# A two-layer decoder trunk on one core: the first norm's row sums by matmul, sixteen hand-over transfers split seven to nine, and the query projection with both activation parts in one 512-column matmul

## The chip, the cores and the metric

The kernel runs on one core of a Trainium2 chip. The metric is device time in microseconds of one execution. Engines are named as in the profile: PE is the matmul engine (PEld its weight loads), DVE the vector engine, ACT the scalar engine, POOL is GpSimd, SP the engine that only issues transfers (POOL and ACT issue some too). A row "L316" points at line 316 of the kernel before.

## The reference, cut to what matters

One sequence of 256 tokens, width 2048, fp32, passes two layers:

```python
for l in range(DEPTH):                    # DEPTH = 2
    h = rms_norm(x, mix_norm[l])
    if l % 2 == 0:
        h = mixer_ab(h, ...)              # gated spatial mixing, and a gated linear recurrence (HGRN2)
    else:
        h = mixer_c(h, ...)               # attention with forget gates, 16 heads
    x = x + h
    h = rms_norm(x, ffn_norm[l])
    x = x + conv_ffn(h, ...)              # up-projection, width-3 causal convolution, SiLU gate, down-projection

def rms_norm(x, gain):
    y = x * lax.rsqrt(jnp.mean(x * x, axis=-1, keepdims=True) + RMS_EPS)
    return y * gain
```

In `mixer_ab` one input projection of the normed x yields six parts u, v, q, f, i, g of 1024 columns each. In the recurrence, each of 8 heads of 128 has queries q, keys from f, values from i; its scores are formed per chunk with a running decay. The division by the root mean square is a factor per token, so the kernel applies it after the projections (except in q, whose scale goes out in the later head norm together with a factor on the outputs).

## The kernel before, in words

**Layout and number format.** x is kept feature-major: 16 tiles `xT[k]` of 128 features x 256 tokens. Every projection is computed to nearly fp32 accuracy from two reduced-precision parts: an operand w is split into `wh` (rounded to the matmul format, by ACT) and `wl = w - wh` (by DVE), and an activation tile `a` of 512 columns holds its high part in columns 0 to 255 and its low part in 256 to 511 (`split`). A product is the sum of three matmuls: high x high, low weight x high activation, high weight x low activation. Weights stream from memory in pieces of 128x1024, 512 KB each, issued on SP and split as they land (`weights`, `halves`, lines 185 and 186); three to five buffers let this run ahead of PE.

**Two kinds of projection.** `project_four` (lines 360 to 362), `project_tok` and `project_first` (lines 260 and 236) keep tokens as rows: the activation is the loaded weight of PE, and 512 columns of the weight matrix stream by. `project` (line 316) keeps features as rows: 128 columns of the weight matrix are loaded, and 256 token columns stream by. It is used for the eight query heads (`w_q[h]`), and for the last four pieces of the final down-projection. Its result, 128 features x 256 tokens, sits in half of a 512-column bank, and two ACT copies (lines 882 and 883) put the first 128 tokens and, reversed, the second 128 into the head's tile `kq[h]`.

**The order of work.** The program text fixes the order on PE. Work of other engines around it (norms, recurrence heads, gates) is written as generators; `tick()`, called ahead of every weight piece, advances up to four or five of them by one step. So a step's place in the program is counted in ticks. `held` and `tied` add orders to keep an operation from being placed ahead of the last weight split or the last matmul. Each engine then runs its queue strictly in order.

**The norms.** A `Norm` object takes each x tile as it becomes final: `feed_split` makes the two parts `a`, scaled by the gain, and `feed_square` adds the squares into `acc` (128 x 256: one partial sum per feature row and token). What is left is the sum over 128 rows for each token. `finish_tok` does it on DVE: a transposition in 32x32 blocks, a sum, four small copies, a sum, four small copies (lines 472 to 479), and then `rsq`, the reciprocal root: a scale (line 425), Ln and Exp on ACT (line 97), a correction on DVE (lines 428 to 430). For the first norm this generator (`finish`) starts in the middle of `project_first`: seven ticks of squares, a free tick, then `finish_tok`. Its result `Rt` is awaited by ACT, which reads the v and f projections out of their banks with it.

**The recurrence.** `hgrn(h)` forms a head's operands on POOL (lines 747, 749, 755), then small matmuls (line 760), a cascade of scalings (lines 774 to 781), score matmuls (lines 788 and 796) and outputs (lines 818 to 820).

**Hand-overs.** At the end of a mixer or of an FFN the result is turned back to feature-major rows in four parts q = 0 to 3: DVE transposes 32x32 blocks into `tmp`, and `moves` carries them to their places by sixteen transfers of 32 KB, alternately on SP and POOL (line 380, eight each). Then x is added to, and the next norm is fed (`add_four` for the mixers, `add_y` for the FFNs). The last part, q = 3, comes right ahead of the next stage's projections, which need the last four `a` tiles.

Of the kernel before, what the change touches and what calls it, by code (L numbers as in the profile page):

```python
# [8 lines left out]
F32 = mybir.dt.float32  # L9
F32R = mybir.dt.float32r  # L10
U16 = mybir.dt.uint16
AF = mybir.ActivationFunctionType
# [3 lines left out]
P = 128  # L16
S = 256
# [38 lines left out]
def tile_trunk(ctx: ExitStack, tc: tile.TileContext, x, pp_d, cst_d, mlev_d, msk_d,  # L56
# [46 lines left out]
    def view(ap, off, *dims):  # L103
        return bass.AP(ap.tensor, ap.offset + off, [list(ap.ap[0])] + [list(d) for d in dims])

    def back(ap):
        return view(ap, P - 1, (-1, P))
# [5 lines left out]
    def bank():  # L113
        return psum["pool"].tile([P, 512], F32, tag="px", name=nm("px"), bufs=psum["banks"])
# [177 lines left out]
    def by_tokens(t, o):  # L292
        return view(t, o, (1, P), (P, 2))

    def to_tokens(ps):
        return view(ps, 0, (2, P), (1, 2))

    def of_tokens(ps, T):
        return view(ps, T, (2, P))

    def project(wsrc, acts, chunks=(8, 8), k0=0, run=2, parts=None):

        ps = pm.tile([P, 512], F32, tag="pm", name=nm("pm"))
        nk = sum(chunks)
        done = 0
        for c in chunks:
            lo = (k0 + done) * P
            if parts is None:
                tick()
            wh, wl = parts or weights(wsrc[:, lo:lo + c * P], c * P)  # L310
            for k1 in range(0, c, run):
                ks = range(k1, min(k1 + run, c))
                for t, os in ((wh, (0, S)), (wl, (0,))):
                    for k in ks:
                        for o in os:
                            deep["last"] = PE.matmul(to_tokens(ps), t[:, k * P:(k + 1) * P],  # L316
                                                     by_tokens(acts[done + k], o),
                                                     start=done + k + o == 0 and t is wh,
                                                     stop=t is wl and done + k == nk - 1)
            done += c  # L320
        return ps
# [54 lines left out]
    def moves(tmp, dst, queues=(nc.sync, nc.gpsimd), rows=range(4)):  # L376
        n = 2 * BLK
        for a in rows:
            for b in range(4):
                queues[(a + b) % len(queues)].dma_start(dst[BLK * b:BLK * (b + 1), :, a * n:(a + 1) * n],  # L380
                                  tmp[BLK * a:BLK * (a + 1), b * 4 * n:(b + 1) * 4 * n]
                                  .rearrange("p (m r) -> p m r", m=4))
# [53 lines left out]
    class Norm:  # L436
# [25 lines left out]
        def feed(self, k):  # L462
            self.feed_split(k)
            self.feed_square(k)

        def finish_tok(self):
            t = cp.tile([P, LANE], F32, tag="Rt", name=nm("Rt"), bufs=2)
            Rt, ssq, r, u, s = (t[:, i:i + n] for i, n in ((0, 2), (2, 2), (8, 8), (16, 32), (48, 8)))
            sq = tp.tile([P, S], F32, tag="sq", name=nm("sq"))
            by_block = view(self.acc, 0, (1, 2), (2 * BLK, 4), (2, BLK)) if self.turn else \  # L470
                self.acc.rearrange("p (t g i) -> p t g i", t=2, i=BLK)
            held(V.transpose(sq.rearrange("p (t g i) -> p t g i", t=2, i=BLK), by_block), "wl")
            held(V.tensor_reduce(r, sq.rearrange("p (c i) -> p c i", i=BLK), AX.X, ALU.add), "wl")
            yield
            for a in range(4):
                held(V.tensor_copy(u[0:BLK, 8 * a:8 * a + 8], r[BLK * a:BLK * (a + 1)]), "wl")
            V.tensor_reduce(s[0:BLK], u[0:BLK].rearrange("p (a c) -> p c a", a=4), AX.X, ALU.add)
            for g in range(4):
                V.tensor_copy(ssq[BLK * g:BLK * (g + 1)], view(s[0:BLK], g, (4, 2)))
            yield  # L480
            rsq(Rt, ssq, D)
            self.Rt = Rt

    def add_four(q, ps, z, tmp, dst, nxt, halves=1, queues=(nc.sync, nc.gpsimd)):
        for T in range(2):
            SC.activation(cols4(z[:, T]), of_rows(ps[T]), AF.Copy)
        blocks(lambda T: z[:, T], tmp)
        moves(tmp, dst, queues, rows=range(4 // halves))

        def rest():  # L490
            if halves == 2:
                yield
                moves(tmp, dst, rows=range(2, 4))
            for _ in range(LAG - 2 * (q == 3)):
                yield
            for i in range(4):
                m = 4 * q + i
                held(V.tensor_tensor(xT[m], xT[m], dst[:, i], ALU.add), "wl")
                nxt.feed(m)
                if q < 3 or i % 2:  # L500
                    yield
            if q == 3:
                for _ in range(WAIT):
                    yield
                yield from nxt.finish_tok()

        queue.append(rest())


    def mixer_ab(norm):  # L510
# [13 lines left out]
        def finish():  # L524
            k = 0
            for n in SQUARES:
                for _ in range(n):
                    norm.feed_square(k)
                    k += 1
                yield  # L530
            yield
            yield from norm.finish_tok()
            bound()

        depth[0] = 4
# [338 lines left out]
        for h in range(NH):  # L874
            if h in (4, 7):
                values(len(itoks))
            while len(kq) <= h:
                tick()
            if h % 4 == 0:
                os_.append(hp.tile([P, 2, 512], F32, tag="o", name=nm("o"), bufs=2))  # L880
            ps = project(w_q[h], A)
            SC.activation(kq[h][:, 2], of_tokens(ps, 0), AF.Copy)
            SC.activation(back(kq[h][:, 1]), of_tokens(ps, 1), AF.Copy)
            queue.append(hgrn(h))
        for j in range(2):
            ps = project_four(w_g[4 * j:4 * j + 4], A, KT)
# [372 lines left out]
    def ffn(l, norm, last):  # L1259
# [69 lines left out]
        def add_y(q, finish):  # L1329
            tmp, zt = room()  # L1330
            near = last and q == 2
            transposed(lambda T: y[:, T, q * 512:(q + 1) * 512], tmp, zt,
                       (nc.sync, nc.gpsimd, SC, nc.gpsimd, nc.sync) if near else (nc.sync, nc.gpsimd))

            def rest():
                for _ in range(3 if near else LAG - 2 * (q == 3)):
                    yield
                for i in range(4):
                    m = 4 * q + i
                    held(V.tensor_tensor(xT[m], xT[m], zt[:, i], ALU.add), "wl")  # L1340
                    if finish:
                        finish_x(m)
                    if not near and (q < 3 or i % 2):
                        yield
                if q == 3 and not last:
                    for _ in range(WAIT):
                        yield
                    yield from nxt.finish_tok()

            queue.append(rest())  # L1350
# [137 lines left out]
```

## Time and profile before

| | us |
|---|---|
| median of 3 runs (lowest, highest) | 2169.11 (2168.81, 2170.22) |
| the profiled execution | 2169.17 |
| its span, from first to last instruction | 2167.4 |
| PE busy | 2161.6 (100%) |
| DVE, ACT, POOL busy | 1609.0, 1311.8, 470.2 |

The clock granted to PE was full (1.0). A row of a timeline reads: start, duration, engine, line and operation, output and inputs, their shapes, how many instructions were merged (x4), and in brackets the idle time before it with what ended it. A row of grouped instructions reads: count, then busy time, mean duration in ns, then idle time before them. Matmuls are pipelined: a row's duration reaches from its start to the modelled end of its last result, and the next one starts well before that. Their rate is read from the distance of their starts.

### The profile page before, as it was taken

The numbers are of one execution on the slowest core, as the hardware profiler recorded it, in microseconds if no ns is written. First come the engines' busy times: TensorE is split into PE (matmuls) and PEld (weight loads), VectorE is DVE, ScalarE is ACT, GpSimd is POOL, SyncE is SP. The second block draws the span as 40 slices with busy tenths as digits, with TensorE's granted clock in tenths as the row PEclk, the third lists the DMA queues.
The fourth block names the chain that finished last, engine by engine and source line by source line (L and its number), as shares of the span: only waits on it lengthen the run. The fifth ranks groups of instructions, "written<-read, shape, count | busy, mean of one in ns | idle before, by whom it ended". The sixth has DMA issues, their size and how long they took to land.

```text
span 2167.4 us, 32437 instructions
## 1 busy us (share of the span) xinstructions
PE 2161.6 (100%) x10858; PEld 1898.7 (88%) x10858; DVE 1609.0 (74%) x2309; ACT 1311.8 (61%) x1903; POOL 470.2 (22%) x869
## 2 busy tenths in 40 slices
PE   9999999999999999999999999999999999999999
PEld 8898888888888888888888888888888888888888
DVE  7888768877567667776987787877787577667766
ACT  6677756666466545654565556766666466456652
POOL 0252231212012002111233443212211012011203
PEclk9999999999999999999999999999999999999999
DMA  8755777777677767776777766787877677766866
GB/s 302 221 169 176 216 227 231 237 231 240 215 217 211 237 206 220 233 227 207 242 234 227 241 206 212 220 246 221 241 227 233 200 235 216 228 213 212 244 212 194
DMA packets 492456, 483.61 MB, mean 223 GB/s; under 512 B 114912, under 2 KB 460144, under 8 KB 492160
## 3 DMA queue, kind: packets, MB, share of 16 engines
q1 hardware_dynamic: 465888, 453.27, 66.3%
q0 software_dynamic: 24960, 26.12, 5.2%
q10 hardware_dynamic: 1440, 2.15, 0.3%
q8 instruction: 85, 1.39, 0.3%
q14 instruction: 83, 0.68, 0.1%
HBM read 435.24 MB, written 2.11 MB: 202 GB/s over the span
## 4 chain that ended last, share of the span: by engine, by line
PE 96%; DVE 2%; DMA 1%; ACT 1%; issue 0%; SPq 0%; DVEq 0%; ACTq 0%
PE pm L361 26%; PE pm L360 26%; PE pm L362 26%; PE pm L341 4%; PE pm L343 4%; PE pm L342 4%; PE pm L316 3%; PE pm L236 1%; DVE wl L186 1%; PE pm L260 0%; DMA kst<-in_msk 0%; ACT wh L185 0%; PE px L1073 0%; PE px L1126 0%; DMA w<-in_w_v 0%
## 5 line engine op out<-in xcount | busy, mean ns | idle before, releaser
L186 DVE TENSOR_TENSOR wl<-w,wh 128x1024 fp32r<-128x1024 f32 (+1 forms) x820 | 993.5, 1220 | 463.7 <-ACT wh L185 450.6
L185 ACT ACTIVATE wh<-w 128x1024 fp32r<-128x1024 f32 (+1 forms) x820 | 857.5, 1050 | 625.1 <-PE pm L362 451.9
L361 PE MATMUL pm<-wl,a 128*128 128x512 f32 x1728 | 655.4, 379 | 0.7 <-DVE wl L186 0.5
L360 PE MATMUL pm<-wh,a 128*128 128x512 f32 x1728 | 655.5, 379 | 0.0
L362 PE MATMUL pm<-wh,a 128*128 128x512 f32 x1728 | 654.9, 379 | 0.0
L380 POOL DMA_DIRECT2D zt<-tmp x415 | 224.6, 549 | 1133.5 <-DVE tmp L373 1056.0
L361 PEld LDWEIGHTS pm<-wl,a 128*128 128x128 f32 x1728 | 326.6, 189 | 48.3 <-DVE wl L186 2.3
L360 PEld LDWEIGHTS pm<-wh,a 128*128 128x128 f32 x1728 | 326.6, 189 | 46.4
L362 PEld LDWEIGHTS pm<-wh,a 128*128 128x128 f32 x1728 | 326.6, 189 | 46.2
L360 PE MATMUL pm<-wh,hid 128*128 128x512 f32 x688 | 260.8, 379 | 0.0
L361 PE MATMUL pm<-wl,hid 128*128 128x512 f32 x688 | 260.8, 379 | 0.0
L362 PE MATMUL pm<-wh,hid 128*128 128x512 f32 x688 | 260.8, 379 | 0.0
L341 PE MATMUL pm<-wh,a 128*128 128x512 f32 x416 | 158.6, 381 | 0.5 <-ACT a L398 0.5
L343 PE MATMUL pm<-wh,a 128*128 128x512 f32 x416 | 157.8, 379 | 0.0
L342 PE MATMUL pm<-wl,a 128*128 128x512 f32 x416 | 157.7, 379 | 0.0
L362 PEld LDWEIGHTS pm<-wh,hid 128*128 128x128 f32 x688 | 130.0, 189 | 18.5
L361 PEld LDWEIGHTS pm<-wl,hid 128*128 128x128 f32 x688 | 130.0, 189 | 18.4
L360 PEld LDWEIGHTS pm<-wh,hid 128*128 128x128 f32 x688 | 130.0, 189 | 18.4
L380 POOL DMA_DIRECT2D turn<-tmp x160 | 86.9, 551 | 211.3 <-DVE tmp L373 178.0
L1294 ACT ACTIVATE conv<-zt,pp 128x256 f32<-128x256 f32 x176 | 95.9, 590 | 58.3 <-DMA zt<-tmp 58.1
L1295 DVE SCALAR_TENSOR_TENSOR conv<-zt,pp,conv 128x255 f32<-128x255 f32 x176 | 80.1, 479 | 41.8 <-ACT conv L1294 24.4
L373 DVE STREAM_TRANSPOSE tmp<-z 128x512 f32<-128x512 f32 x120 | 98.7, 859 | 6.0 <-ACT z L1280 4.2
(259 smaller groups left out, 2212.6 us busy)
## 6 DMA issues: line engine op xcount, KB each, us to landing
w<-in_w_up SPq DMA_DIRECT2D x352, 512.0 KB, 5.1
w<-in_w_dn SPq DMA_DIRECT2D x176, 512.0 KB, 5.0
w<-in_w_cqkv SPq DMA_DIRECT2D x96, 512.0 KB, 4.7
w<-in_w_abo SPq DMA_DIRECT2D x32, 512.0 KB, 5.0
w<-in_w_cg SPq DMA_DIRECT2D x32, 512.0 KB, 4.9
w<-in_w_co SPq DMA_DIRECT2D x32, 512.0 KB, 4.8
zt<-tmp POOLq DMA_DIRECT2D x415, 32.0 KB, 2.5
zt<-tmp SPq DMA_DIRECT2D x414, 32.0 KB, 2.7
```

The costliest lines, as they stand in the source:

```text
L185: r = deep["wh"] = SC.activation(wh, w, AF.Copy)
L186: deep["wl"] = V.tensor_tensor(wl, w, wh.bitcast(F32), ALU.subtract)
L341: PE.matmul(to_two(ps[T]), ah, h, start=k + i == 0, stop=False)
L342: PE.matmul(to_two(ps[T]), ah, l, start=False, stop=False)
L343: deep["last"] = PE.matmul(to_two(ps[T]), al, h, start=False, stop=k + i == KT - 1)
L360: PE.matmul(to_rows(ps[T]), ah, h, start=not begun and k + i == ks[0], stop=False)
L361: PE.matmul(to_rows(ps[T]), ah, l, start=False, stop=False)
L362: deep["mm"] = deep["last"] = PE.matmul(to_rows(ps[T]), al, h, start=False, stop=not more and k + i == ks[-1] + 1)
L373: V.transpose(tmp.rearrange("p (b m i t) -> p b m i t", b=4, m=4, t=2)[:, :, :, :, T], src(T).rearrange("p (m b j) -> p b m j", m=4, b=4))
L380: queues[(a + b) % len(queues)].dma_start(dst[BLK * b:BLK * (b + 1), :, a * n:(a + 1) * n], tmp[BLK * a:BLK * (a + 1), b * 4 * n:(b + 1) * ...
L1294: held(SC.activation(c, z, AF.Identity, bias=pp[:, cb:cb + 1], scale=w(2)))
L1295: V.scalar_tensor_tensor(c[:, 1:], z[:, :S - 1], w(1), c[:, 1:], ALU.mult, ALU.add)
```

## The change

Three edits.

1. **Queries.** `project` gets a mode `fold`, used for the eight heads' queries. The high weight part is loaded once per k-block and meets both parts of the activation in one matmul of 512 columns (high part's tokens in columns 0 to 255, low part's in 256 to 511 of the bank); the low weight part meets the high part as before, in columns 0 to 255. The two halves must then be added. ACT copies each into a tile of 128x256 (`tag="sq"`, the tag of the norms' squares), and POOL adds them, once for the first 128 tokens and once, reversed, for the second.

2. **First norm.** `finish_first` stands in place of `finish_tok` for the first norm alone: two matmuls with the sums `acc` as loaded weights and two columns of ones, each giving the totals of 128 tokens. They are ordered behind the last matmul recorded in `deep["mm"]`. After two more ticks `rsq` reads them from the bank.

3. **Transfers.** At q = 3 of both mixers' and both FFNs' hand-overs, the sixteen transfers go by the list `SEVEN` of length seven, indexed by a + b: seven on SP, nine on POOL. Other parts keep the alternation.

```diff
+                if fold:
+                    for k in ks:
+                        PE.matmul(ps, wh[:, k * P:(k + 1) * P], view(acts[done + k], 0, (S, 2), (1, P), (P, 2)),
+                                  start=done + k == 0, stop=False, skip_group_check=True)
+                    for k in ks:
+                        deep["last"] = PE.matmul(to_tokens(ps), wl[:, k * P:(k + 1) * P],
+                                                 by_tokens(acts[done + k], 0),
+                                                 start=False, stop=done + k == nk - 1, skip_group_check=True)
+                    continue
...
+        def finish_first(self):
+            p2 = bank()
+            for T in range(2):
+                r = PE.matmul(p2[:, 2 * T:2 * T + 2], self.acc[:, T * P:(T + 1) * P], ones[:, 0:2],
+                              start=True, stop=True)
+                if "mm" in deep:
+                    tc.add_manual_dep(r.ins, deep["mm"].ins.name, order, reason="not before")
+            Rt = cp.tile([P, LANE], F32, tag="Rt", name=nm("Rt"), bufs=2)[:, 0:2]
+            yield
+            yield
+            rsq(Rt, p2[:, 0:4].rearrange("p (t two) -> p t two", two=2)[:, :, 0], D)
+            self.Rt = Rt
...
+    SEVEN = (nc.sync, nc.gpsimd, nc.sync, nc.gpsimd, nc.gpsimd, nc.sync, nc.sync)
...
-        moves(tmp, dst, queues, rows=range(4 // halves))
+        moves(tmp, dst, SEVEN if q == 3 else queues, rows=range(4 // halves))
...
-            yield from norm.finish_tok()
+            yield from norm.finish_first()
...
-            ps = project(w_q[h], A)
-            SC.activation(kq[h][:, 2], of_tokens(ps, 0), AF.Copy)
-            SC.activation(back(kq[h][:, 1]), of_tokens(ps, 1), AF.Copy)
+            ps = project(w_q[h], A, fold=True)
+            z = [tp.tile([P, S], F32, tag="sq", name=nm("z")) for _ in range(2)]
+            for i in range(2):
+                SC.activation(z[i], ps[:, i * S:(i + 1) * S], AF.Copy)
+            for i, q in enumerate((kq[h][:, 2], back(kq[h][:, 1]))):
+                nc.gpsimd.tensor_tensor(q, view(z[0], i, (2, P)), view(z[1], i, (2, P)), ALU.add)
...
-                       (nc.sync, nc.gpsimd, SC, nc.gpsimd, nc.sync) if near else (nc.sync, nc.gpsimd))
+                       (nc.sync, nc.gpsimd, SC, nc.gpsimd, nc.sync) if near else
+                       SEVEN if q == 3 else (nc.sync, nc.gpsimd))
```

More of the change, by code (lines that the diff above doesn't have):

```diff
@@ L299, in of_tokens, with project @@
         return view(ps, T, (2, P))
-    def project(wsrc, acts, chunks=(8, 8), k0=0, run=2, parts=None):
+    def project(wsrc, acts, chunks=(8, 8), k0=0, run=2, parts=None, fold=False):
         ps = pm.tile([P, 512], F32, tag="pm", name=nm("pm"))
```

## The prediction

> **What bounds the kernel now.** I read the page first (busy times, then the chain that ended last), then the waits of the matmul engine (PE), then its timeline.
>
> ```profile
> PE 2161.6 (100%) x10858; PEld 1898.7 (88%) x10858; DVE 1609.0 (74%) x2309; ACT 1311.8 (61%) x1903; POOL 470.2 (22%) x869
> PE 96%; DVE 2%; DMA 1%; ACT 1%; issue 0%; SPq 0%; DVEq 0%; ACTq 0%
> PE pm L341 <- ACT a L398: 0.5, 1, 0.5
> PE pm L361 <- DVE wl L186: 0.5, 1, 0.5
> ```
>
> The first line is from the page: PE is busy for all but 5.8 us of a span of 2167.4. The second is the chain of waits, 96% of it matmuls. The last two are from the view of PE's waits: once the start-up is over it waits twice, 0.5 us each. So whatever this change does on the other engines is worth at most a few us, unless it opens new gaps on PE. What counts is the number of PE nanoseconds, and those two places.
>
> A busy PE hides the rate, because a matmul's row lasts longer than its turn. The turn is the distance between starts, from the timeline of PE at the border of `project_four` (512 columns) and `project` (256 columns):
>
> ```profile
> 87.67 0.38 PE L362 MATMUL pm<-wh,a 128*128 128x512 f32 x1
> ...
> 89.61 0.38 PE L362 MATMUL pm<-wh,a 128*128 128x512 f32 x1
> 89.83 0.61 PE L316 MATMUL pm<-a,wh 128*128 128x256 f32 x4
> ...
> 92.50 1.06 PE L585 MATMUL px<-wt,gv 128*128 128x128 f32 x8
> 93.31 0.69 PE L316 MATMUL pm<-a,wh 128*128 128x256 f32 x4
> ```
>
> From 87.67 to 89.61 there are nine turns of 512 columns: 215.6 ns each. From 89.83 to 92.50 there are 24 turns of 256 columns (eight k-blocks of three): 111.3 ns each. Both are almost pure streaming; what a matmul pays beyond its columns is small.
>
> **Part 1: queries in one 512-column matmul.** The group's rows give the count:
>
> ```profile
> L316 PE MATMUL pm<-a,wh 128*128 128x256 f32 x256 | 39.7, 278 | 0.0
> L316 PE MATMUL pm<-a,wl 128*128 128x256 f32 x128 | 24.7, 275 | 0.0
> ```
>
> That is 8 heads x 16 k-blocks x 3. Per k-block, three turns of 111.3 (333.9 ns) become one of 215.6 and one of 111.3 (326.9 ns): 7.0 ns saved, and over 128 k-blocks **-0.9 us**. The columns are the same in number; only a fixed cost per instruction goes. The new moving operand (two halves, each read with a stride) has as many dimensions as the one that `project_four` reads at 215.6. Beside the row, the Trainium skill, page "TensorE: Matmul & The Clock Gate", section "Back-to-back issue gap", gives columns/2.4 + 2.5 ns a turn; by that, an estimate, the saving would be 2.5 ns a block or 0.3 us in all. The 512-column row agrees with it (215.8); the 256-column row stands 2 ns above it, and the measurement decides.
>
> The price is on the other engines. Per head, two ACT copies out of PSUM of 128x128 become two of 128x256, and two GpSimd (POOL) adds are new:
>
> ```profile
> 146.80 0.28 ACT L882 ACTIVATE kq<-pm 128x128 f32<-128x128 f32 x1
> 147.13 0.39 ACT L822 ACTIVATE o<-px 128x256 f32<-128x256 f32 x1
> 148.50 0.51 POOL L747 TENSOR_TENSOR kd<-kd,kq 128x128 f32<-128x128 f32 x1 [3.61 <-ACT kd L746]
> 149.10 0.52 POOL L749 TENSOR_TENSOR kq<-kq,lf 128x128 f32<-128x128 f32 x1
> 151.17 0.33 PE L760 MATMUL px<-kq,kd 128*32 128x32 f32 x16
> 157.49 1.23 DVE L186 TENSOR_TENSOR wl<-w,wh 128x1024 fp32r<-128x1024 f32 x1
> 157.74 1.35 POOL L747 TENSOR_TENSOR kd<-kd,kq 128x128 f32<-128x128 f32 x1 [0.87 <-ACT kd L746]
> ```
>
> ACT: 0.39 - 0.28 = 0.11 more per copy, 0.2 us a head, in a stage whose ACT rows show it waiting for PE. POOL: an add of this size is L747 or L749, 0.51 to 1.35 us, so 1.0 to 2.7 us a head. Behind the adds, on POOL's queue, stand L747 and L749 of the same head, and PE's L760 needs their result: in the tight case above POOL ends at 149.62 and PE starts L760 at 151.17, 1.55 us of cover. In front of the adds POOL sat idle for 3.61 us, waiting for the ACT copy `kd`, so a part of the adds falls into that idle time. I take **0**. The bound upward is an add pair of 2.7 + 0.2 against 1.55, with about 0.6 falling into idle time: 0.7 us at each of the three heads whose cover I found to be this short, +2.1 us; downward nothing, since no PE instruction gets earlier data. Bank release is no issue: the copies read all of the bank within 0.8 us, and the next project starts 2.7 us or more later.
>
> A rule speaks against this part. The 1.35 us row of L747 began 0.25 us after a DVE `wl` with two SBUF inputs and ended 0.37 us after it; without such a neighbour the same operation took 0.51. The Trainium skill, page "SBUF — State Buffer", section "Who interferes with whom", states just that: a DVE instruction with two SBUF inputs and a GpSimd one that reads SBUF exclude each other, and whoever comes second is blocked entirely. By that, the trace agrees; it is the mechanism of the slower rival below.
>
> **Part 2: the first norm by matmuls.** Timelines of DVE, ACT and PE:
>
> ```profile
> 40.70 0.95 DVE L459 TENSOR_TENSOR acc<-acc,sq 128x256 f32<-128x256 f32 x2
> 44.65 0.44 DVE L472 STREAM_TRANSPOSE sq<-acc 128x256 f32<-128x256 f32 x1
> 48.66 1.41 DVE L476 COPY Rt<-Rt 32x8 f32<-32x8 f32 x4
> 52.49 0.67 DVE L479 COPY Rt<-Rt 32x2 f32<-32x2 f32 x4
> 53.27 0.16 DVE L425 TENSOR_SCALAR rm<-Rt 128x2 f32<-128x2 f32 x1
> 53.47 0.20 ACT L97 ACTIVATE Rt<-rm 128x2 f32<-128x2 f32 x1 [2.23 <-DVE rm L425]
> 53.92 1.28 ACT L93 ACT_TABLE_LOAD   x1
> 56.50 1.05 ACT L185 ACTIVATE wh<-w 128x1024 fp32r<-128x1024 f32 x1
> 47.39 0.38 PE L360 MATMUL pm<-wh,a 128*128 128x512 f32 x1
> 55.16 0.38 PE L360 MATMUL pm<-wh,a 128*128 128x512 f32 x1
> 55.47 0.48 PE L361 MATMUL pm<-wl,a 128*128 128x512 f32 x1
> 57.95 0.38 PE L360 MATMUL pm<-wh,a 128*128 128x512 f32 x1
> 58.86 0.48 PE L361 MATMUL pm<-wl,a 128*128 128x512 f32 x1 [0.53 <-DVE wl L186]
> ```
>
> The sums are ready at 41.65, yet the old finish (eleven small DVE operations from 44.65 to 53.16, mixed with weight splits) lets `rm` start only at 53.27. ACT's Ln waits 2.23 us for it, and the weight split behind it on ACT's queue starts at 56.50. So two weight pieces are late on PE: at 55.16 the next start comes 0.31 instead of 0.216 later, and at 57.95 0.91 later; each first matmul after the gap lasts 0.48 instead of 0.38, another 0.10 before the following turn. Together 0.09 + 0.10 + 0.70 + 0.10 = 0.99 us.
>
> After the change, two matmuls of 128x128 weights and 2 columns stand on PE behind the first piece of `w_f` (emitted at the ninth tick, that is behind k = 0, which ends 12 turns of 215.6 after 47.39, at 50.0). Their input has been ready for 8 us, so PE does not wait. `rm` then starts at about 51 or, if DVE takes the split at 51.3 first, at 52.5; Ln, Exp and table load (0.2 + 0.2 + 1.28) end by 52.9 to 54.4, a gelu of 0.7 later the split `wh` follows, and `wl` is done by 55.7 to 57.3, before 57.97, when PE wants it. The piece at 55.16 is freed too, since eleven operations leave DVE. So both gaps close: **-1.0 us**, bounds -1.0 and 0. What is late next here is PE itself.
>
> The price on PE: fp32 matmuls appear as two records each, so four records. The L585 rows above took 0.81 us for eight, 101 ns each, and the four L316 behind them lasted 0.69 instead of 0.61, 0.08 us late. Low end: sixteen records of L760 in 0.33 us, 0.08 for four. With full 128x128 weights the nearest row is L585: 4 x 0.10 + 0.08 = **+0.5 us**; ends 0.1 and 0.6.
>
> **Part 3: seven to nine transfers.** In each q = 3 hand-over SP issues 7 instead of 8, POOL 9. There are four such places; only one has a PE wait behind it (the L341 wait quoted first), from the FFN of layer 0 to the attention:
>
> ```profile
> 1046.86 5.12 SPq L380 DMA_DIRECT2D zt<-tmp  x8
> 1047.12 4.33 POOL L380 DMA_DIRECT2D zt<-tmp  x8 [5.98 <-DVE x L1340]
> 1051.37 3.46 DMA zt<-tmp
> 1055.45 1.10 DVE L1340 TENSOR_TENSOR x<-x,zt 128x256 f32<-128x256 f32 x3 [0.62 <-DMA w<-in_w_cqkv]
> 1056.95 0.38 PE L343 MATMUL pm<-wh,a 128*128 128x512 f32 x1
> 1057.88 0.48 PE L341 MATMUL pm<-wh,a 128*128 128x512 f32 x1 [0.55 <-ACT a L398]
> zt<-tmp POOLq DMA_DIRECT2D x415, 32.0 KB, 2.5
> ```
>
> SP needs 0.64 us an issue; its last landed 3.46 us after 1051.37 (row of the chain), and DVE, idle for 0.62 us, then added x; PE's next start came 0.93 instead of 0.216 later, 0.7 us lost and 0.25 in restarts. Without the eighth, SP is done 0.64 earlier. POOL's ninth issues at 1047.12 + 8 x 0.54 = 1051.4 and lands after 2.5 (the median of the page) to 3.46: 1053.9 to 1054.9. DVE gains 0.6 at best (busy until 1055.45 - 0.62 = 1054.83) and loses 0.1 at worst. Between the ends I take **-0.4 us** on PE; bounds -0.9 (a gap of which only restart remains) and +0.1. At the other three places PE shows no wait, so half a microsecond more on POOL is covered by the pieces of work ahead; SP's weight loads behind the transfers get 0.64 us earlier.
>
> **Sum.** -0.9 + 0 - 1.0 + 0.5 - 0.4 = -1.8 us. The profiled execution took 2169.17 (span 2167.4 and 1.8 around it), 0.06 above the median of three runs, 2169.11, so the sum holds for the median too: **2167.4 us**, 0.08% less. What a measurement of this kernel can tell from no change is about 0.2%, 4.3 us: I forecast no change that shows.
>
> **Rivals.**
> *Nothing gained (2169.1).* The closed gaps reopen behind another wait, or POOL's ninth transfer is the new last one. For it: the 51 to 53 us window leaves `rm` little choice, and the ninth issue at 1051.4 is as late as SP's eighth was. Then -0.9 + 0.5 and some tenths: 2168.5 to 2169.6.
> *Slower: POOL's adds and DVE's splits lock each other.* Between 88 and 200 us both are much used, and each of the 16 adds may wait out a split of 1.23 us or hold one up. Price: the add pair reaches 2.7 us a head; it decides from the point where the pair and the copies exceed the 1.55 us (plus idle time) ahead of L760. At three heads that gives +2.1 (2169.5); if every head lost 0.8, 6.4 us: 2173.8. Against it: most heads leave POOL microseconds idle (3.61 us before 148.50), and the splits run ahead of PE.
> *Faster by more.* Both gaps close entirely and the norm's matmuls cost 0.1: -0.9 - 1.0 + 0.1 - 0.9 = -2.7, 2166.4. To get beyond 0.2% (below 2164.8) would need a gain that no row shows: the page's 5.8 us of idle PE lie mostly in the start-up.
>
> **How the numbers follow.** Forecast (2166.4 to 2168.4) 0.60; nothing gained (to 2169.7) 0.20; locking adds (above 2169.7) 0.15, a third of that beyond 2173.4; more gained 0.05, of which 0.03 beyond 2164.8. A range from 2166.0 to 2170.4 leaves out about 0.04 below and 0.12 above. So faster 0.03, within 0.2% 0.92, slower 0.05.
>
> **What would show it.** Part 1: 128 rows of 128x512 at L316's place with turns of 0.216, and no PE wait on POOL before the 32-row matmuls; a PE wait for `kq` or a longer stretch from 88 to 200 us would prove it wrong. Part 2: `rm` before 52.6, no gap near 55 and 58 us, four short records near 50 us. Part 3: the L343 to L341 step near 1056 shorter than 0.93. The forecast is wrong if any PE wait above 1 us appears, most likely behind POOL.

## The result, and the profile after

| | before | after |
|---|---|---|
| median (lowest, highest), us | 2169.08 (2168.23, 2170.69; one of 3835.65 is left out) | 2173.15 (2170.92, 2176.45) |
| the profiled execution | 2169.17 | 2173.14 |
| PE, DVE, ACT, POOL busy | 2161.6, 1609.0, 1311.8, 470.2 | 2162.1, 1606.4, 1314.2, 487.0 |

Both are medians of 21 executions. The ratio is 1.0018, with an interval of 1.0012 to 1.0023: the change makes the kernel 4.1 us slower. The forecast was 2167.4, between 2166.0 and 2170.4. The sign was wrong, and the range missed.

First the changed kernel's page, then its view of PE's waits (total us, how often, the longest):

```profile
PE 2162.1 (100%) x10734; PEld 1899.8 (87%) x10734; DVE 1606.4 (74%) x2298; ACT 1314.2 (61%) x1903; POOL 487.0 (22%) x889
PE 94%; DVE 2%; ACT 1%; issue 1%; POOL 1%; DMA 0%; DVEq 0%; ACTq 0%; POOLq 0%
```

```profile
PE px L784 <- POOL kq L773: 2.1, 1, 2.1
PE pm L350 <- ACT a L407: 1.4, 1, 1.4
PE pm L351 <- DVE wl L186: 0.5, 1, 0.5
```

The second line of the first block is the chain of work that ended last, by engine. PE's busy total hardly moved, and the shares of the chain say little. The waits say it: where two waits of 0.5 us stood, there are now 2.1, 1.4 and 0.5. The old lines L760, L747, L749, L746 and L341 are now L784, L771, L773, L770 and L350.

**The largest wait: the last head (h = 7).** First the timelines of ACT, POOL and PE before, then those of the changed kernel with DVE's (L908 copies a half of the bank, L910 is POOL's sum, L770 the copy `kd`, L771 and L773 the two products behind it):

```profile
189.99 0.28 ACT L882 ACTIVATE kq<-pm 128x128 f32<-128x128 f32 x1
191.94 0.84 POOL L749 TENSOR_TENSOR kq<-kq,lf 128x128 f32<-128x128 f32 x1
193.59 0.38 PE L818 MATMUL px<-itok,st 128*128 128x128 f32 x2
194.35 0.33 PE L760 MATMUL px<-kq,kd 128*32 128x32 f32 x16
```

```profile
189.94 0.38 ACT L908 ACTIVATE z<-pm 128x256 f32<-128x256 f32 x1
190.76 1.62 DVE L858 TENSOR_TENSOR o<-o,small 128x512 f32<-128x512 f32 x2
191.03 1.72 POOL L910 TENSOR_TENSOR kq<-z,z 128x128 f32<-128x128 f32 x2 [0.45 <-ACT z L908]
192.78 0.34 ACT L770 ACTIVATE kd<-kq 128x128 f32<-128x128 f32 x1 [0.25 <-POOL kq L910]
193.05 1.25 DVE L186 TENSOR_TENSOR wl<-w,wh 128x1024 fp32r<-128x1024 f32 x1
193.20 1.47 POOL L771 TENSOR_TENSOR kd<-kd,kq 128x128 f32<-128x128 f32 x1 [0.45 <-ACT kd L770]
194.74 0.51 POOL L773 TENSOR_TENSOR kq<-kq,lf 128x128 f32<-128x128 f32 x1
192.42 0.39 PE L842 MATMUL px<-itok,st 128*128 128x128 f32 x2
195.31 0.33 PE L784 MATMUL px<-kq,kd 128*32 128x32 f32 x16 [2.06 <-POOL kq L773]
```

Read the brackets. ACT's copy `kd` (L770) waits for POOL's sums (L910), although it needs only the keys of that tile. The copy reads two key parts of `kq` through one strided view whose extent spans the query part between them, so it is ordered behind the sums. What used to be two POOL products has become a row: copies, sums, `kd`, product, product. From the first copy to the end of the last product it took 2.79 us before (189.99 to 192.78) and takes 5.31 now. The copies also come later against PE: before, the first copy began 3.60 us ahead of the matmuls of L818, now 2.48 ahead of the same ones (L842). The cover that the prediction spoke of, 1.55 us, was here 1.57 (192.78 to 194.35). 2.52 + 1.12 - 1.57 = 2.07 us, the wait that the profile shows.

**What it costs after it has ended.** The windows of the changed kernel (busy time of PE, PEld, DVE, ACT and POOL, then PE's granted clock, the DMA share and GB/s) before the wait, 1 us and 5 us after PE's restart, and three rows of PE's timeline:

```profile
190.00:192.00 2.00, 2.00 (x11) 1.76 (x11) 1.90 (x6) 1.96 (x7) 1.47 (x4) 1.00 0.56 159
196.40:199.20 2.80, 2.80 (x8) 2.23 (x7) 1.94 (x5) 2.47 (x7) 0.00 (x0) 0.50 0.77 246
200.00:202.00 2.00, 2.00 (x11) 1.76 (x10) 1.28 (x2) 1.49 (x3) 0.00 (x0) 1.00 0.74 212
```

```profile
196.32 0.63 PE L369 MATMUL pm<-wh,a 128*128 128x512 f32 x1
196.75 0.63 PE L370 MATMUL pm<-wl,a 128*128 128x512 f32 x1
199.73 0.38 PE L371 MATMUL pm<-wh,a 128*128 128x512 f32 x1
```

From 196.32 to 199.73 there are eight turns of 427 ns where a turn is 216: another 1.7 us. The clock granted in that stretch is 0.50. A column for busy time shows nothing of it, PE is busy throughout. The Trainium skill, page "TensorE: Matmul & The Clock Gate", section "What's actually happening", says that the array drops to half its clock after an idle window of about 3.4 us and regains it after about 3.4 us of work. The trace agrees with the second (about 3.4 us at 0.50) and differs in the first: here 2.06 us without a matmul were enough.

The trace's record of the granted clock shows more. It changes only on a raster of 3.413 us: full for 56 such steps, half for one (196.31 to 199.73), full for 578. In the step that ended at 196.31, PE had been idle for 2.06 of the 3.41 us. The wait of 1.44 us at 1061, described next, also lay within one step, and the clock stayed full. So in these traces it is the idle share of a fixed step that counts, with the limit somewhere between 1.44 and 2.06 us.

**The second: the hand-over ahead of the attention.** Timelines of SP, POOL, DVE and PE:

```profile
1049.43 4.47 SPq L389 DMA_DIRECT2D zt<-tmp  x7
1054.01 3.75 SPq L198 DMA_DIRECT2D w<-in_w_cqkv  x5
1049.70 4.87 POOL L389 DMA_DIRECT2D zt<-tmp  x9 [5.99 <-DVE x L1368]
1058.92 1.10 DVE L1368 TENSOR_TENSOR x<-x,zt 128x256 f32<-128x256 f32 x3 [1.52 <-issue]
1059.53 0.38 PE L352 MATMUL pm<-wh,a 128*128 128x512 f32 x1
1061.35 0.48 PE L350 MATMUL pm<-wh,a 128*128 128x512 f32 x1 [1.44 <-ACT a L407]
```

SP finished its transfers a turn earlier and at once began its 512 KB weight loads at 1054.01; POOL's ninth went out at 1054.02 and landed at 1058.84 by its semaphore, 4.8 us later, where most of them took about 2. PE's turn here is 1.82 us instead of 0.93. The 1.52 us before DVE's row, marked "issue" since the view names no cause for them, end with this landing.

**What worked.** PE's timeline at the fold, 1.96 us for three pairs of k-blocks (0.653 a pair), then PE, DVE and ACT at the first norm:

```profile
183.34 0.38 PE L318 MATMUL pm<-a,wl 128*128 128x256 f32 x2
183.56 0.60 PE L315 MATMUL pm<-a,wh 128*128 128x512 f32 x2
185.30 0.39 PE L318 MATMUL pm<-a,wl 128*128 128x256 f32 x2
```

```profile
49.40 0.50 PE L478 MATMUL px<-ones,acc 128*128 128x2 f32 x4
49.76 0.46 PE L369 MATMUL pm<-wh,a 128*128 128x512 f32 x1
50.06 0.38 PE L370 MATMUL pm<-wl,a 128*128 128x512 f32 x1
52.26 0.15 DVE L434 TENSOR_SCALAR rm<-px 128x2 f32<-128x2 f32 x1
54.78 1.05 ACT L185 ACTIVATE wh<-w 128x1024 fp32r<-128x1024 f32 x1
```

The norm's matmuls take 0.36 us and 0.08 in the next turn, `rm` starts at 52.26 instead of 53.27, the split at 54.78 instead of 56.50, and no gap is left near 55 and 58 us.

**The account**, from the distances of PE's starts, us: fold -0.9; norm -0.99 + 0.44 = -0.55; last head's turn 2.30 longer than the usual one where it was 0.17, so +2.13; half clock +1.69; a new wait for `wl` at 170.54 (L350 to L351), +0.77 with the restart; hand-over 1.60 instead of 0.71, +0.89. Sum +4.0; the profiled executions differ by 3.97. That the two agree so well is partly luck, because the sum leaves out two things that nearly cancel. In this execution PE's stream stood 0.59 us earlier than before by 17 us already, in the start-up, which no edit touches (a1 below: 0.34 earlier, b2: 0.34 later). And from the start of PE's last matmul to the end of the span it took 4.13 us instead of 3.72, +0.41; all kernels with the list of seven and nine show this (4.12 or 4.13), and the others have 3.69 to 4.00, so it seems to belong to the transfers.

### The profile page after: what moved, and what is told of

Same layout as the page of the kernel before. It is cut to its first block, busy times and chain, and to the rows that moved or that the text cites. A ratio compares the mean times of both kernels' runs of the same rounds, so it can differ in the third digit from the quotient of the medians.

```text
span 2171.4 us, 32197 instructions
## 1 busy us (share of the span) xinstructions
PE 2162.1 (100%) x10734; PEld 1899.8 (87%) x10734; DVE 1606.4 (74%) x2298; ACT 1314.2 (61%) x1903; POOL 487.0 (22%) x889
## 4 chain that ended last, share of the span: by engine, by line
PE 94%; DVE 2%; ACT 1%; issue 1%; POOL 1%; DMA 0%; DVEq 0%; ACTq 0%; POOLq 0%
PE pm L370 26%; PE pm L369 26%; PE pm L371 26%; PE pm L350 4%; PE pm L351 4%; PE pm L352 4%; PE pm L236 1%; DVE wl L186 1%; PE pm L315 1%; PE pm L260 1%; PE pm L325 0%; ACT wh L185 0%; DVE kq L802 0%; PE pm L318 0%; PE px L1100 0%
## 5 line engine op out<-in xcount | busy, mean ns | idle before, releaser
L350 PE MATMUL pm<-wh,a 128*128 128x512 f32 x416 | 158.8, 382 | 1.4 <-ACT a L407 1.4
L351 PE MATMUL pm<-wl,a 128*128 128x512 f32 x416 | 158.0, 380 | 0.5 <-DVE wl L186 0.5
```

Of the source, the lines that this page charges most:

```text
L350: PE.matmul(to_two(ps[T]), ah, h, start=k + i == 0, stop=False)
L351: PE.matmul(to_two(ps[T]), ah, l, start=False, stop=False)
```

## The experiments

My theory had three places: the fold's saving is real but its sums make PE wait in the last head; that wait drags PE's clock down; transfers that go out beside the weight loads land late. The first four kernels take the change apart, and try the nearest rival for the last head (POOL's adds, which DVE locks out).

**a1: the fold alone.** The old norm and old transfers put back:

```diff
-            yield from norm.finish_first()
+            yield from norm.finish_tok()
...
-        moves(tmp, dst, SEVEN if q == 3 else queues, rows=range(4 // halves))
+        moves(tmp, dst, queues, rows=range(4 // halves))
```

> The queries' fold alone (GpSimd adds), old first norm, old eight-to-eight transfers. Theory: in the last head the chain of ACT copy, two POOL adds, ACT kd copy and two POOL products ends about 195.2 us, while PE, 0.9 us ahead through the fold, wants the 32-column matmuls at about 193.4: a PE wait of 1.3 to 1.9 us there, and after it several 512-column matmuls at half rate (+1.7 us). Sum -0.9 + 1.6 + 1.7 = about +2.4, 2171.5 us, with a wider spread of runs than before. Rival (the wait needs the lead that the first norm gives PE): no half rate, 2168 to 2169 us.

Measured: 2172.47 against 2169.6, ratio 1.0013 (1.0004 to 1.0022). PE's 32-row matmuls (L784) start at 196.19 after a wait of 2.06 us for POOL, and eight slow turns follow, most of 427 ns. PE came only 0.3 us earlier than before at this place, so the wait doesn't need the norm's gain; but the copies again began 2.48 us ahead of L842.

**a2: the norm alone.**

> The first norm by matmuls alone. Theory: the waits near 55 and 58 us close (-1.0), four short records cost +0.4, and the start-up is as before: 2168.5 us. Rival (PE's lead is taken back at the next place where POOL is late): 2169.1 us, with a new PE wait of some tenths before a group of 32-column matmuls.

Measured: 2168.86, 0.9996 (0.9987 to 1.0005), 0.7 below the kernel before. The interval contains 1, so the times alone don't show a gain; in the trace the gaps near 55 and 58 us are closed.

**a3: the transfers alone.**

> The seven-to-nine transfers alone. Theory (the ninth POOL transfer shares the DMA engines with the 512 KB weight loads that SP now starts 0.64 us earlier): the step from layer 0's FFN to the attention waits 0.9 us longer than before, 2170.0 us. Rival (the longer wait in the changed kernel came from its other parts): -0.4 us, 2168.7 us.

Measured: 2171.22, 1.0008 (1.0000 to 1.0017), 1.6 above. POOL's last transfer and SP's first weight load both went out at 1051.75; the transfer took 4.3 us, and PE's turn was 1.27 us at 1057. The profiled execution was the fastest of the eleven (2170.35); in it this turn is 0.34 longer than before and the stretch behind PE's last matmul 0.41, and where the rest of the 1.6 lies is not shown. The three parts by themselves give +2.9, -0.7 and +1.6, +3.8 in all, about what the whole gives.

**a4: the whole change, halves summed by DVE out of the bank.**

```diff
-            for i in range(2):
-                SC.activation(z[i], ps[:, i * S:(i + 1) * S], AF.Copy)
+            SC.activation(z, ps[:, S:2 * S], AF.Copy)
...
-                nc.gpsimd.tensor_tensor(q, view(z[0], i, (2, P)), view(z[1], i, (2, P)), ALU.add)
+                V.tensor_tensor(q, of_tokens(ps, i), view(z, i, (2, P)), ALU.add)
```

> The whole change, but the two halves are added by DVE straight from the bank (one ACT copy of the low half, then two DVE sums of a bank half and an SBUF half), so nothing new stands on POOL. Theory: the PE wait of 2.06 us in the last head and the half rate behind it vanish, and the wait near 170 us shrinks; what is left is the transfers' +0.9: 2173.1 - 2.1 - 1.7 - 0.4 = about 2169 us. Rival (the fold itself or DVE's load is the cost): 2172 us or more.

Measured: 2173.46, 1.0018 (1.0010 to 1.0027): a miss. Timelines of ACT, POOL and PE:

```profile
191.79 0.32 ACT L770 ACTIVATE kd<-kq 128x128 f32<-128x128 f32 x1 [0.32 <-DVE kq L909]
192.19 1.34 POOL L771 TENSOR_TENSOR kd<-kd,kq 128x128 f32<-128x128 f32 x1 [2.26 <-ACT kd L770]
195.25 0.33 PE L784 MATMUL px<-kq,kd 128*32 128x32 f32 x16 [2.65 <-POOL kq L773]
```

With no add on POOL the wait is longer still. POOL now idles for 2.26 us for `kd`, which waits for the sums, whoever makes them (the second one stands on DVE's queue behind the two rows of L858). So POOL's adds are not needed for the wait. The rows show two things at once: `kd` starts late, and the two products then run beside DVE's weight splits and take 1.34 and 1.58 us (L771, L773) instead of about 0.5. This sent me to the order of `kd`.

**b2: the whole change, with eight idle matmuls to fill PE's wait.** They read ones and write an unused part of a bank, ahead of head 7's 32-row matmuls:

```diff
+            if h == NH - 1:
+                for _ in range(8):
+                    tied(PE.matmul(dg[:, S:S + P], ones, ones, start=True, stop=True))
```

> The whole change, with eight idle matmuls (ones by ones, into unused columns of the bank) ahead of the last head's 32-column matmuls: PE is busy for 1.8 of the 2.06 us that it waits for POOL. POOL's chain is as before. Theory (PE's half rate behind the wait comes from the idle time itself): the 427 ns turns vanish, -1.7 us against the whole change, about 2171.4 us, and the runs' spread shrinks. Rival (the half rate comes from something that runs at that time on the other engines): the slow turns stay, 2173.1 us.

Measured: 2171.24 against 2169.32, 1.0010 (1.0001 to 1.0019): 1.9 above the kernel before, where the whole change is 4.1 above. Windows and timeline of PE:

```profile
197.20:200.20 3.00, 3.00 (x15) 2.62 (x15) 1.62 (x3) 2.14 (x5) 0.00 (x0) 1.00 0.75 231
```

```profile
194.41 1.95 PE L784 MATMUL px<-ones 128*128 128x128 f32 x16
196.66 0.33 PE L787 MATMUL px<-kq,kd 128*32 128x32 f32 x16 [0.30 <-POOL kq L773]
1589.79 0.48 PE L370 MATMUL pm<-wl,a 128*128 128x512 f32 x1 [1.70 <-DVE wl L186]
```

PE still loses as long at this place, but works meanwhile, and the clock stays at 1.00. So the half clock is the price of the idle time, 1.7 us by the turns. The 2 us between the medians are no second proof: in its trace PE loses nothing at the hand-over, although the list of transfers is the same. There POOL's ninth went out at 1053.68, 0.98 us ahead of the first weight load (1054.66), landed after 1.8 us, and PE did not wait. The last row, a chance wait of 1.70 us late in the same run, is followed by turns of the usual length; by the clock's raster it fell into two steps, 1.41 us of it into the first.

**c1: sums on DVE, and `kd` apart.** As a4, with the copy and the product in two parts each, so that the key part no longer spans the queries:

```diff
-            SC.activation(view(kd, 0, (P + 1, 2), (2, H)), view(t, 0, (3 * P + 1, 2), (2, H)), AF.Copy)
-            nc.gpsimd.tensor_tensor(kb, kb, view(t, 1, (3 * P - 1, 2), (2, H)), ALU.mult)
+            for i in range(2):
+                SC.activation(view(kd, i * (P + 1), (2, H)), view(t, i * (3 * P + 1), (2, H)), AF.Copy)
+            for i in range(2):
+                kbi = view(kd, 1 + i * (P - 1), (2, H))
+                nc.gpsimd.tensor_tensor(kbi, kbi, view(t, 1 + i * (3 * P - 1), (2, H)), ALU.mult)
```

> The whole change with the sums on DVE, and the ACT copy and the POOL product that form a head's kd cut in two each, so that neither touches the query half of the tile and neither waits for the sums. Theory (kd was only late because it was ordered behind the query sums, and then met DVE's weight splits): in the last head kd's products start near 191 us, no PE wait over 0.5 us there, no half rate: 2173.5 - 2.7 - 1.7 = about 2169 us. Rival (POOL's chain is late by itself, whatever it waits for): 2172 us or more.

Measured: 2170.27, 1.0005 (0.9996 to 1.0014): 0.95 above the kernel before, where a4, which differs in these lines alone, was 3.86 above. Timelines of ACT, POOL and PE:

```profile
188.80 0.44 ACT L771 ACTIVATE kd<-kq 128x64 f32<-128x64 f32 x2 [0.19 <-DVE kd L769]
190.52 0.66 POOL L774 TENSOR_TENSOR kd<-kd,kq 128x64 f32<-128x64 f32 x2
193.57 0.33 PE L787 MATMUL px<-kq,kd 128*32 128x32 f32 x16 [0.27 <-POOL kq L776]
```

`kd` starts 3 us earlier than in a4, the wait falls from 2.65 to 0.27, and there are no half-rate turns. That shows that without the order of `kd` there is no long wait in the last head. It doesn't separate the order from the slow products, because `kd`'s products, once early, also ran clear of the splits (0.66 us for both parts); nor was `kd` set apart with POOL's sums. The expectation of about 2169 was missed: PE's trace has a new wait for a split right behind (turn 0.82 at 193.84), one at 170.94 (0.55), and at the hand-over a turn of 1.76 us, where a4 had 1.50.

**d2: the kernel before with nine transfers on SP and seven on POOL.**

```diff
-    SEVEN = (nc.sync, nc.gpsimd, nc.sync, nc.gpsimd, nc.gpsimd, nc.sync, nc.sync)
+    SEVEN = (nc.gpsimd, nc.sync, nc.gpsimd, nc.sync, nc.sync, nc.gpsimd, nc.gpsimd)
```

> The kernel before with the q = 3 transfers the other way round: nine on SP, seven on POOL. Theory (the last transfer is late when it is issued as the 512 KB weight loads start, and SP alone keeps those loads behind its transfers): SP's ninth issues 0.64 us later and lands as late after its issue as the eighth did, +0.6 us: 2169.7 us. Rival (POOL's transfers are the slow ones): the wait shrinks by up to 0.7 us, 2168.5 us.

Measured: 2169.29, 1.0001 (0.9992 to 1.0009). No loss, where I had expected 0.6: PE's turn at the hand-over fell to 0.50 us.

**e1: the norm, and a list with one transfer on ACT.** The last entry of `SEVEN` is `SC`; in the trace SP issued six, POOL nine and ACT one.

> The first norm by matmuls, no fold, and the q = 3 transfers seven on SP, eight on POOL, the last on ACT. Theory: the norm's gain stands (-0.7), and no transfer is left to be issued together with the weight loads, so the wait between layer 0's FFN and the attention falls from 0.93 to some tenths: 2168.1 us. Rival (ACT's queue holds its transfer back behind a weight split): the wait grows, 2169 us or more.

Measured: 2174.13, 1.0021 (1.0013 to 1.0030): a miss by 6 us, and the run with the latest transfer. ACT's transfer was not the late one: it went out first, at 1046.14, and landed after 2.3 us. Its timelines of SP and PE, a piece of its chain, and its windows:

```profile
1050.07 4.39 SPq L198 DMA_DIRECT2D w<-in_w_cqkv  x5
1059.70 0.80 PE L350 MATMUL pm<-wh,a 128*128 128x512 f32 x1 [3.08 <-ACT a L407]
```

```profile
1050.19 4.37 DMA zt<-tmp
1054.55 2.72 issue
```

```profile
1050.00:1056.00 6.00, 6.00 (x29) 5.27 (x28) 4.11 (x6) 1.88 (x4) 1.27 (x3) 1.00 0.89 278
1060.50:1065.00 4.50, 4.50 (x12) 3.50 (x12) 4.34 (x9) 3.81 (x6) 1.14 (x2) 0.50 0.51 155
```

SP was free still earlier, so the weight loads began at 1050.07. POOL's last transfer went out behind them, at 1050.72, and landed 6.5 us later by its semaphore, at 1057.19. (The chain names the transfer before it; its 2.72 us of "issue" end with this landing.) PE waited 3.1 us and then ran at half clock for twelve turns.

The kernels so far give a row: the last transfer issued 0.7 us ahead of the first weight load took 3.5 us (before, a2), at the same time 4.3 (a3) and 4.8 (after), 0.65 behind it 6.5 (e1). The 3.5 us have another cause than the rest, as told at the end of the next section.

**g1: the norm, with nine transfers on SP** (a2 and d2 together).

> The first norm by matmuls, queries as before, and the q = 3 transfers dealt the other way round: nine on SP, seven on POOL. My theory of the hand-over: a small transfer that is issued at the time when SP's 512 KB weight loads start, or after it, lands late (3.4 us when 0.7 ahead of them, 4.3 to 4.8 at the same time, 6.5 when 0.65 behind), because the loads take the DMA engines; with nine on SP the weights start 0.64 later and POOL's last goes out about 1.5 us ahead of them, so every one lands in under 3 us. Then the wait near 1057 shrinks to 0.5 or less (turn under 0.55 instead of 0.93), the gaps near 55 and 58 us are closed as with the norm alone (2168.86), and the time is 2168.2 to 2168.6, ratio 0.9995. Rival (the place of the sixteenth transfer is what counts, not the weights): SP's ninth is late by as much as POOL's ninth was, the turn near 1057 is 1.3 us or more, and the time 2169.3 or above.

Measured: 2168.49 against 2169.34, 0.9998 (0.9989 to 1.0006). At the hand-over POOL's last landed after 1.8 us, as expected, and PE's turn was 0.41 us. But not every transfer landed in under 3 us: SP's eighth, 1.34 us ahead of the weights, took 3.5. (The landing of its ninth, 0.70 ahead, is not told by the trace.) And the gain over a2 is only 0.1 by the two differences. Timelines of SP and DVE at another q = 3 hand-over, from the mixer to the first FFN, and PE's waits from 300 to 400 us:

```profile
361.15 7.01 SPq L389 DMA_DIRECT2D dst<-tmp  x9
369.99 1.10 DVE L522 TENSOR_TENSOR x<-x,dst 128x256 f32<-128x256 f32 x3 [0.82 <-DMA dst<-tmp]
```

```profile
PE pm L370 <- DVE wl L186: 0.5, 1, 0.5
```

Here SP's nine are the late ones (in a2 eight took 6.11 us and x was added at 369.29), and a turn near 374 is 0.64 us too long. d2 shows the same, 0.58. Neither list suits all four places.

**f2: the fold without its sums.** The kernel before with the 512-column matmul; one half is read out as before, and the high weight x low activation product is left out of the queries.

> The kernel before with the 512-column matmul alone: one half of the bank is read out (as before, two ACT copies of 128x128), and the other half, the product with the activations' low parts, is left out of the queries. So the PE gain stands by itself, with nothing new on ACT, DVE or POOL. My theory: 128 turns of 0.327 instead of 0.334 per k-block give -0.9 us, and with no sums ahead of kd no wait appears at the last head's 32-row matmuls: 2168.4 to 2168.7, ratio 0.9996. Rival (PE that arrives earlier at the last head waits by itself, whatever the sums do): a wait of about 1 us for POOL near 194 us, and 2169.3 or above.

Measured: 2168.44, 0.9996 (0.9987 to 1.0005): 0.9 below, the size of PE's saving, though the interval contains 1. There is no wait in the last head, and the copies start 3.87 us ahead of L842 (3.60 before). So what goes wrong in the fold is the sums and what is ordered behind them.

**f1: the whole change, mended** (c1 with nine on SP).

> The whole change with its two faults mended: the halves of the queries added by DVE out of the bank (one ACT copy of one half left), the ACT copy kd and the POOL product with it each in two parts so that the key part does not stand behind the query sums, and nine transfers on SP, seven on POOL. With the first two mendings and seven on SP it took 2170.27, with a wait of 0.5 at the last head's 32-row matmuls, 0.6 behind a DVE split, and 1.55 + at the hand-over near 1057. If the three losses add up, nine on SP takes 1.0 to 1.3 us off: 2169.0 to 2169.3, and no PE wait above 0.7 us is left. Rival (the losses do not add, another wait takes the place): within 0.3 us of 2170.27.

Measured: 2168.59, 0.9995 (0.9987 to 1.0004): 0.75 below the kernel before, and 4.8 better than the whole change (+4.07). The losses add up, and more: against c1 it is 1.7 us, where 1.0 to 1.3 were expected.

**h1: g1, and the fold with POOL's sums in heads 0 to 6 only.**

```diff
+            ps = project(w_q[h], A, fold=h < 7)
```

> The first norm by matmuls, nine transfers on SP and seven on POOL, and the fold with POOL's sums in heads 0 to 6, while the last head (h = 7) projects its queries as before. My theory: the whole loss of the fold, 2.3 us of wait and 1.7 of half-rate turns, sits at the last head, where no other work stands between the projection and the 32-row matmuls; heads 0 to 6 have the cover and keep 7/8 of the 0.9 us. Then no PE wait above 1 us is left between 88 and 200 us, and the time is 2167.4 to 2167.9, ratio 0.9992: 0.8 below the same kernel without the fold. Rival (the sums lock with DVE's splits at other heads too, which the loss at the last head only hid): a wait for POOL or for a split of 0.5 us or more at another head, and 2168.6 or above.

Measured: 2168.73, 0.9997 (0.9988 to 1.0006): a miss by 0.8 us, on the rival's side. The 2.1 us wait is gone, and the half clock with it, but PE's timeline has a new gap in the last head:

```profile
193.24 0.48 PE L369 MATMUL pm<-wh,a 128*128 128x512 f32 x1
194.18 0.48 PE L370 MATMUL pm<-wl,a 128*128 128x512 f32 x1 [0.46 <-DVE wl L186]
```

A turn of 0.94 here and one 0.40 too long at 170.45, with 0.1 each in the restart, give back 1.3 us: more than the fold saves in seven heads. Neither is seen in g1, which has no fold, or in f2, which has no sums. So the sums seem to make DVE's splits late here too: POOL's last step ahead of the copies (L779) began at 188.45, against 187.97 in g1, while PE arrived 0.5 us earlier.

No version is shown to beat the kernel before: g1, f1, h1 and f2 all have intervals that contain 1. g1, f1 and h1 are 4.7 to 4.9 us faster than the changed kernel, by their differences to the kernel before.

## Why the prediction was wrong, point by point

- **What bounds the kernel**: right. PE's nanoseconds and its waits decided; all of the result but the 0.4 us behind PE's last matmul are turns of PE that can be pointed at. The least change that can be told was put too high, at 0.2%: the interval of the result is 0.11% wide, and 0.18% stands clear of no change.
- **Fold, -0.9**: right in size (0.653 us a pair of k-blocks in the trace, and -0.9 between the medians of f2).
- **The price of the fold, "I take 0"**: the step that failed. It let a part of the adds fall into POOL's idle time ahead of them, "waiting for the ACT copy `kd`". But `kd` itself waits for the sums: the idle time moved behind them and the steps became a row. Its upper bound, +2.1 for three heads, meets the one wait (+2.13 in one head) by chance. The sum took 0 for what measured +2.13 and its consequences. It held nothing for the clock afterwards (+1.69) or for splits that come late elsewhere (+0.77 near 170 us). ACT's 0.2 us a head and the cover of 1.55 us were read rightly.
- **"Locking adds"**, given 0.15, named the place and the right order of price, 2169.5 to 2173.8. The rows of L910 beside L858 and of L771 beside `wl` (1.47 us, against 0.51 for L773 with no such neighbour) show the slowdown that it spoke of: about 1.6 us in all, if the sums would take 0.5 each without it. But a4 has no POOL add and waits longer, and c1 takes the wait away by order alone. So the order puts the steps in a row and in the way of the splits, and the splits lengthen them; how much of the 2.06 us each would cost by itself is not shown.
- **Norm, -1.0 + 0.5**: right: -0.99 + 0.44 in the trace, -0.7 in a2. (The time "57.97, when PE wants it" is in no row; PE reached that piece at 57.95.)
- **Transfers, -0.4**: wrong in sign, +0.9 at the hand-over and +0.4 behind PE's last matmul in the trace, +1.6 in a3. The ninth POOL transfer was given 2.5 to 3.46 us to land and took 4.8: 2.5 is the page's median over 415 transfers, and the 3.46 were SP's eighth, which had left 0.7 us ahead of the weight loads. That "SP's weight loads behind the transfers get 0.64 us earlier" was written down as a gain and is what made it late. The lower end, +0.1, rested on the same rows.
- **"Nothing gained"** and **"faster by more"** did not happen.
- **What would show it**: Part 2's signs came as described. Part 1's rows came too, but with the PE wait for `kq` that was to prove it wrong, and Part 3's step grew to 1.82 us. The last sentence, a wait above 1 us "most likely behind POOL", is what occurred.

The late transfers can be explained further. The Trainium skill, page "DMA: Bandwidth & Descriptors", section "Issuing engines are not separate DMA queues", says that transfers of all issuers share the same sixteen engines and interleave. The DMA share of 0.89 in the window of e1 fits that. The traces also hold the single DMA packets, and these say more. In e1 the sixteen 2 KB packets of POOL's last transfer began between 1054.48 and 1055.95, 3.8 to 5.2 us after its issue, and fifteen of them within 10 ns of the end of a 4-byte packet of SP's queue, the kind that ends a weight load's share. In the changed kernel they ran between the weights' 4 KB packets, fifteen from 1056.30 to 1057.05 and the last at 1058.07. So the packets waited for DMA engines that carried the weights. DVE also ran splits back to back at that time; no run excludes that it adds something.

The 3.5 us are another matter. A transfer's semaphore counts sixteen shares. Before the change, fifteen shares of SP's last had come at 1053.25, the usual 1.9 us after its issue; the sixteenth came at 1054.84. Its packets began at 1053.79, just as a 16 KB packet of an instruction queue ended (1052.75, 1.05 us long). In g1 such a packet ran from 1052.98 to 1054.24 and the late share began at 1054.23, a microsecond ahead of the first weight packet (1055.23). In h1, and in b2 while the last transfers were out, no such packet ran, and PE had no wait there. So a late sixteenth is tied to that packet by time; no run moves it alone.

## What to carry to other kernels

Before an operation is placed ahead of others on a queue, follow who waits for its output tile, by the extent of each reader's view and not by the elements that it reads: a reader of another part may be tied to it. A transfer that ends a stage needs a lead over the next stage's bulk loads (0.98 us in b2 was enough, none in a3 was not), so freeing the queue that issues those loads can cost more than the shorter queue saves. And price a new PE wait of 2 us at up to twice its length: read the granted clock behind it.

## What the runs showed of the hardware that I had not expected

- PE's clock: waits of 2.06 us (a1, after), 2.65 (a4) and 3.08 (e1) each came with a granted clock of 0.50, the first three for 3.41 us and the last for 6.83, which began while PE still waited. The idle time inside the 3.413 us step before was 2.06, 2.06, 2.50 and 2.28 us. Waits of 1.44 us (after, at 1061) and 1.70 (b2, 1.41 of it in one step) left the clock full. A wait of 2.2 us filled with idle matmuls left it full too.
- A 32 KB transfer that lands in about 2 us at this hand-over took 4.3 to 4.8 us when issued together with the 512 KB loads (a3, after) and 6.5 when issued 0.65 us behind the first (e1). POOL's median over the whole kernel hardly shows it: 2.5 us before, 2.6 after.
- One of a transfer's sixteen shares came 1.6 us behind the other fifteen (before, SP's last) when a 16 KB packet of an instruction queue ran at that moment.
